# A decoder block's attention stage: probabilities turned in the order of their banks, queries requested two blocks ahead, a new written order, and the second output weights requested sooner

## The chip, the cores and the metric

The kernel runs on one core of a Trainium2 chip. The metric is the device time of one execution in microseconds (us); lower is better. Times of a kernel are medians over several runs. One execution of the kernel before was recorded by the hardware profiler, and all times of single instructions come from it.

## The reference: what is computed

One layer of a decoder block for a sequence of 2048 positions with 1024 channels, in float32. A projection feeds three groups of heads (a matrix memory, eight heads of forgetting attention, a spatial gate); their outputs are joined and multiplied by an output matrix, added to the input, and a convolutional feed-forward network follows. The change lies in the forgetting attention and in the output matrix that follows it:

```python
def forgetting_attention(q, k, v, f_pre):
    F = jnp.cumsum(jax.nn.log_sigmoid(f_pre.astype(jnp.float32)), axis=-1)
    for blk in range(s_len // Q_BLOCK):          # Q_BLOCK = 128
        lo, hi = blk * Q_BLOCK, (blk + 1) * Q_BLOCK
        logits = (jnp.einsum('bhtd,bhsd->bhts', qb, kb) * scale
                  + F[:, :, lo:hi, None] - F[:, :, None, :hi])
        logits = jnp.where(mask, logits, -jnp.inf)   # causal
        p = jax.nn.softmax(logits, axis=-1)
        outs.append(jnp.einsum('bhts,bhsd->bhtd', p, vb))
...
    y = jnp.concatenate([y_attn, y_mlstm, y_sgu], axis=-1)
    return y @ w_out
...
        x = x + gt1 * y
```

## The kernel before

The program has four stages: projections (to about 690 us of the span), attention (to 1084.6 us), the output matrix (to about 1260 us) and the feed-forward network (to the end). The change touches the second and the third.

**Attention.** Eight heads `h` of 64 channels; each has four blocks `tb` of 512 queries, worked on in the order 0 to 3 (head 0: 3, 2, with 1 and 0 done earlier; head 7: 2, 3, 0, 1). A block has four tiles `i` of 128 queries. Each step of the work is a letter of the string `order`, and the engines get their instructions in that order (a manual schedule):

- `S` (`score`): TensorE multiplies one query tile with up to 1024 keys into a pair of PSUM banks (`pair()`, three such pairs in turn, `pb` twice and `pc` once); VectorE adds the forget bias and keeps the row minimum (line 223), which writes `L`.
- `X` (`weigh`): ScalarE takes the exponential of `L` (line 231), GpSimd divides by the row sum (lines 232 and 233).
- `T`, `U`, `W` (`turn_pair`): TensorE transposes two key tiles of probabilities into a PSUM pair, 64 queries at a time, the lower half of the queries in one bank and the upper half in the other (line 246); the pair is copied to `pT` in SBUF. The letter says who copies: `T` ScalarE one half and VectorE the other, `U` ScalarE alone (line 260), `W` VectorE alone (line 262). The copy puts the two halves of each query tile side by side, in runs of 64. A pair on the diagonal (`p >= tb * 2`) is copied in two instructions, one per key tile.
- `V` (`value_pair`): two matmuls of `pT` with the values into the halves of a PSUM bank `op` (line 270).
- `Y`, `Z` (`leave`): VectorE or ScalarE copies `op` to `yo`, and SyncE writes it to two tensors in DRAM (line 286).
- `a`: one split of an output weight or of one of the joined outputs `y` into a rounded high and a low part (`split_parts`, lines 135 and 136), for the next stage.

All transfers are issued by one queue, SyncE's (SP in the profile), in the order of the program: where one has to wait for its data or its buffer, those behind it wait too. The queries of a block (`load_q`, line 189: four transfers of 128 KB) are requested at the first `S` of the block before, into four buffers `qB`, which hold two blocks. At a head's first block the keys of the next head follow them (`load_k`: four transfers of 256 KB and 1 MB of forget bias), and for each second head 1 MB of values (`load_v`).

**Output matrix.** For each block of 512 positions (`TBS`, so 2, 3, 0, 1), eight steps `j` of 24 matmuls: four row tiles with the weights' first 512 columns (`wo0`), then the same four with the second 512 (`wo1`), in the first block in that order (`by_nb`). The weights `wo0` and seven of the eight parts `y` of the first block are split during attention, by the letters `a`. Part 3 of `y`, and the weights `wo1` with their gain (`load_w(1, gt1...)`), are requested in the stage itself. All these loads go through three buffers `ld`. Four PSUM banks take the sums, so a step's sums must have been moved when the step four later begins.

Of the kernel before, what the change touches and what calls it, by code (L numbers as in the profile page):

```python
# [17 lines left out]
P = 128  # L18
# [15 lines left out]
def trunk(  # L34
# [202 lines left out]
    def turn_pair(h, tb, p, how):  # L237
        tp = pair()
        i0 = max(0, 2 * p - tb * 4)
        for j in (2 * p, 2 * p + 1):  # L240
            for i in range(max(0, j - tb * 4), 4):
                n_p = min(8, tb * 4 + i + 1 - j // 8 * 8)
                o = j // 8 * 1024 + (place(j % 8) - 4 + (n_p + 1) // 2) * P
                at = j % 2 * 256 + i * 64
                for f, r in enumerate((lower, upper)):
                    T.transpose(tp[:, f, at : at + 64], L_[h, tb, i][0][r, o : o + P], ident[r, r])
        pT = pT_[h, tb, p] = pool.tile([P, 1024], F32, name="pT", tag="pT")
        if p < tb * 2:
            src = [tp.rearrange("p f (n c) -> p f n c", c=64)]
            dst = [pT.rearrange("p (n f c) -> p f n c", f=2, c=64)]  # L250
            if how == "T":
                src, dst = [src[0][:, f] for f in range(2)], [dst[0][:, f] for f in range(2)]
        else:
            src, dst = [], []
            for j, i in ((0, i0), (1, i0 + 1)):
                src.append(tp[:, :, j * 256 + i * 64 : j * 256 + 256].rearrange("p f (i c) -> p f i c", c=64))
                dst.append(pT[:, j * 512 + i * P : j * 512 + 512].rearrange("p (i f c) -> p f i c", f=2, c=64))
        for n, (d, t) in enumerate(zip(dst, src)):
            if how == "U" or how == "T" and n == 0:
                A.copy(d, t)  # L260
            else:
                V.tensor_copy(d, t)

    def value_pair(h, tb, p):
# [3 lines left out]
        for j in (2 * p, 2 * p + 1):  # L268
            c0 = max(0, j - tb * 4) * P
            T.matmul(  # L270
                op_[h, tb][(lower, upper)[j % 2], c0:], vv_[h // 2][:, j, h % 2 * 64 : h % 2 * 64 + 64],
                pT[:, j % 2 * 512 + c0 : j % 2 * 512 + 512], start=p == 0, stop=p == 2 * tb + 1,
            )

    def leave(h, tb, how):
        op = op_.pop((h, tb))
        yo = pool.tile([P, 512], F32, name="yo", tag="yo")
        copy = V.tensor_copy if how == "Y" else A.copy
        if tb:
            copy(yo, op)  # L280
        else:
            copy(yo[lower], op[lower])
            copy(yo[upper, P:], op[upper, P:])
# [1052 lines left out]
    def y_split(n=9):  # L1336
# [6 lines left out]
        "USUSTSSUXVSSSXSVVXTXSSSVVTSSVSZUTSTYXXSVVVTUTWVXSSXSSSSXXXSVVXWTTSXUTVVTTSSSVSXSXSXSVXVSXTSXSSVXVZVT"  # L1343
        "TTSYXSUVVVTTTXZSSSTVVXVVVSSSXTSSXUVTZTSXXSSSVXXVXVSTWUSXVSTTSXUSVVWXXSSSVVXTSXSSSVXVVTUTSSSWZZXVVVVX"
        "TSSTSUSXSSZSXTVVXVTTXXSUSXVVVXVXYVSTTUSSVTTUXSSVYVXVTTSSSXVVVXVZTTTTXSSSXSVVVTTSXSSUVVXSZSSSSXSVXVTT"
        "UXSWVVVXTTTUSXSTVVXSZTXSSSVXXVSTSYSXTVVXVUTSSXSXVVVTTTSZSSXSVXVVVTUSWZUVVXSSXSXWTWXVVVVXYUSUXSSSSXXS"
        "VVXVXSTTSUVTSXSUTVTTSXSSSYVVVTXSSSSXVVVVXTTTYSSSVXXVVTTTTUVYTSSXXSXSSSXVXVVTTTSXSSXVZXVSWSVVSXXTTUSW"
        "VVTSXSSXSVVTTXSXSSSVYVUSXTTVYVVTTSXSSVVYXVSTTUSUVVYWXSXSSXaWVVWTSaVVVZSaUWWVVTTXSSSVVXSSSXVTSXSaUVXV"
        "SSaSWWaUVVaXVWSXSZTaVXaVXVTTTVVUSSSWXZXXaVXVVWaUaUVVVVTTYaUWaUVVYaVVVVZ"
# [776 lines left out]
```

## Time and profile before

| what | value |
|---|---|
| median of 3 runs | 2553.86 us (2552.37 to 2555.32) |
| the profiled execution | 2552.41 us, span 2550.4 us |
| mean granted TensorE clock | 0.992 |
| DVE (VectorE) busy | 1898.0 us (74%) |
| ACT (ScalarE) busy | 1193.5 us (47%) |
| POOL (GpSimd) busy | 382.2 us (15%) |
| packets of the data queue q1 | 45.7% of 16 engines' time |

How to read it: PE is TensorE, PEld its weight loads, SPq the queue that issues the transfers. The span is the time from the first to the last instruction. A wait is named after what ended it. An engine's idle time costs something only where others wait for it; TensorE is busy nearly all the time, so its own idle time and its slowed clock are what to look at first.

### The profile page before, as it was taken

The numbers are of one execution on the slowest core, as the hardware profiler recorded it, in microseconds if no ns is written. First come the engines' busy times: TensorE is split into PE (matmuls) and PEld (weight loads), VectorE is DVE, ScalarE is ACT, GpSimd is POOL, SyncE is SP. The second block draws the span as 40 slices with busy tenths as digits, with TensorE's granted clock in tenths as the row PEclk, the third lists the DMA queues.
The fourth block names the chain that finished last, engine by engine and source line by source line (L and its number), as shares of the span: only waits on it lengthen the run. The fifth ranks groups of instructions, "written<-read, shape, count | busy, mean of one in ns | idle before, by whom it ended". The sixth has DMA issues, their size and how long they took to land.

```text
span 2550.4 us, 39158 instructions
## 1 busy us (share of the span) xinstructions
PE 2478.5 (97%) x14361; PEld 1992.3 (78%) x14361; DVE 1898.0 (74%) x3249; ACT 1193.5 (47%) x2119; POOL 382.2 (15%) x421
## 2 busy tenths in 40 slices
PE   6999999999998989999999999999999999999999
PEld 6888888888755555578878888888888888888887
DVE  7657656576275667855599888888888888988897
ACT  5443343433376656635465444444444444444443
POOL 2023310233265455500000000000000000000000
PEclk9999999999999999999999999999999999999999
DMA  7335753455555343466723222264222219577523
GB/s 264 112 117 161 221 146 94 126 153 149 144 150 146 92 112 96 121 215 235 263 91 108 83 83 83 83 252 145 83 83 83 83 66 314 169 245 255 169 75 120
DMA packets 288792, 369.27 MB, mean 145 GB/s; under 512 B 31086, under 2 KB 181580, under 8 KB 287576
## 3 DMA queue, kind: packets, MB, share of 16 engines
q1 hardware_dynamic: 288600, 366.77, 45.7%
q8 instruction: 113, 1.85, 0.3%
q14 instruction: 79, 0.65, 0.1%
HBM read 270.15 MB, written 96.54 MB: 144 GB/s over the span
## 4 chain that ended last, share of the span: by engine, by line
PE 48%; DVE 2%; DMA 1%; ACT 1%; issue 0%; SPq 0%; POOL 0%; ACTq 0%; DVEq 0%
PE ub L54 11%; PE ub L56 11%; PE ub L55 11%; PE db L55 5%; PE db L56 5%; PE db L54 5%; DMA hc_d<-hl 1%; DMA x_d<-x 0%; DVE T L1530 0%; DVE B L1530 0%; DVE hz L1521 0%; DVE wspl L1586 0%; ACT hz L1500 0%; ACT T L1526 0%; SPq L351 0%
## 5 line engine op out<-in xcount | busy, mean ns | idle before, releaser
L54 PE MATMUL acc<-wh,hh 128*128 128x512 f32 (+2 forms) x752 | 279.6, 373 | 0.0
L54 PE MATMUL ub<-T,wsph 128*128 128x512 f32 x704 | 273.8, 389 | 1.2 <-ACT wsph L1582 1.2
L55 PE MATMUL ub<-T,wsph 128*128 128x512 f32 x704 | 274.3, 390 | 0.2 <-DVE T L1530 0.2
L56 PE MATMUL ub<-T,wspl 128*128 128x512 f32 x704 | 273.9, 389 | 0.0
L56 PE MATMUL acc<-wh,hl 128*128 128x512 f32 (+2 forms) x752 | 269.8, 360 | 0.2 <-DVE hl L596 0.2
L55 PE MATMUL acc<-wl,hh 128*128 128x512 f32 (+2 forms) x752 | 268.8, 359 | 0.6 <-DVE wl L638 0.6
L54 PE MATMUL db<-wsph 128*128 128x512 f32 x616 | 239.5, 389 | 0.0
L55 PE MATMUL db<-wspl,wsph 128*128 128x512 f32 x616 | 239.5, 389 | 0.0
L56 PE MATMUL db<-wsph,wspl 128*128 128x512 f32 x616 | 239.5, 389 | 0.0
L1582 ACT CAST wsph<-S 128x512 fp32r<-128x512 f32 x176 | 109.3, 623 | 218.8 <-PE ub L55 153.8
L55 PE MATMUL ub<-B,wsph 128*128 128x512 f32 x528 | 205.6, 389 | 1.0 <-DVE B L1530 0.9
L54 PE MATMUL ub<-B,wsph 128*128 128x512 f32 x528 | 205.7, 390 | 0.0
L56 PE MATMUL ub<-B,wspl 128*128 128x512 f32 x528 | 205.5, 389 | 0.0
L1725 ACT CAST wsph<-act 128x512 fp32r<-128x512 f32 x154 | 96.1, 624 | 229.9 <-PE db L55 219.9
L223 DVE CUSTOM_DVE_ANT_0 L<-pr,nf 128x1024 f32<-128x1024 f32 (+7 forms) x128 | 124.3, 987 | 77.7 <-PE pr L217 42.8
L217 PE MATMUL pr<-kk,q 64*128 64x512 f32 (+3 forms) x1104 | 148.0, 371 | 27.2 <-DMA q<-q_d 19.5
L231 ACT ACTIVATE L<-L,nm 128x1792 f32<-128x1792 f32 (+15 forms) x128 | 153.5, 1203 | 22.7 <-DVE nm L223 21.9
L56 PEld LDWEIGHTS acc<-wh,hl 128*128 128x128 f32 x752 | 142.4, 190 | 21.8 <-DVE hl L596 0.4
L55 PEld LDWEIGHTS acc<-wl,hh 128*128 128x128 f32 x752 | 142.9, 190 | 19.9 <-DVE wl L638 1.5
L54 PEld LDWEIGHTS acc<-wh,hh 128*128 128x128 f32 x752 | 142.8, 190 | 19.1 <-issue 0.5
L54 PEld LDWEIGHTS ub<-T,wsph 128*128 128x128 f32 x704 | 132.1, 188 | 28.8 <-ACT wsph L1582 1.6
L55 PEld LDWEIGHTS ub<-T,wsph 128*128 128x128 f32 x704 | 132.1, 188 | 28.8 <-DVE T L1530 1.6
(338 smaller groups left out, 5580.1 us busy)
## 6 DMA issues: line engine op xcount, KB each, us to landing
w<-in_w_up_dram SPq DMA_DIRECT2D x88, 512.0 KB
wd<-in_w_down_dram SPq DMA_DIRECT2D x154, 256.0 KB
wa<-in_w_ada_dram SPq DMA_DIRECT2D x96, 256.0 KB
act_d<-yc SPq DMA_DIRECT2D x44, 512.0 KB
act<-act_d SPq DMA_DIRECT2D x44, 512.0 KB
wr<-in_w_in_dram SPq DMA_DIRECT2D x64, 256.0 KB
q<-q_d SPq DMA_DIRECT2D x128, 128.0 KB
hc_d<-hl SPq DMA_DIRECT2D x28, 512.0 KB
```

Source lines behind the costliest of these rows:

```text
L54: T.matmul(ps, lh, rh, start=start, stop=False, skip_group_check=resume)
L55: T.matmul(ps, lh, rl, start=False, stop=False, skip_group_check=resume)
L56: T.matmul(ps, ll, rh, start=False, stop=stop, skip_group_check=resume)
L217: T.matmul(dst, q2[a][r, qs], kk[b][r, ks], start=n == 0, stop=n == 2 and not (last and f == own))
L223: V.tensor_tensor_reduce(out=L[:, c * 1024 : c * 1024 + w], in0=sp[:, o : o + w], in1=nf[:, c * 1024 + o : c * 1024 + o + w], scale=-1.0, ...
L231: A.activation(L, L, AF.Exp, bias=nm[:, n : n + 1], scale=-1.0, accum_out=rs)
L1582: A.copy(self.wa[p][0], self.source(p))
L1725: A.copy(hi, v)
```

## The change

Four things are changed.

- **Turning.** The transposes of a diagonal pair are packed without holes, and `pT` keeps the order of the PSUM banks: first all lower halves (512 columns), then all upper halves. Each copy is then one instruction for all letters and pairs, with long runs. The value matmuls read two runs of 256 columns (fewer on the diagonal) where they read 512 in one, and write `op` in the same order; where a diagonal pair leaves columns out, their destination is two runs. `leave` puts the halves side by side again when it copies `op` to `yo`.
- **Queries.** At a block's first `S` the queries of the next two blocks are requested, if they have not been. `qB` has six buffers and `pT` five.
- **Order.** A new string; it has 58 `T`, 69 `U` and 33 `W` where there were 100, 38 and 22, the same numbers of `S`, `X` and `V`, and one `a` more, for part 3 of `y`. All low parts of `wo0` are made by VectorE; before, GpSimd made every second.
- **Second output weights.** `load_w(1, ...)` stands behind the first step of the first block, where it stood ahead of the fifth; in the first block the parts of `y` for the second are requested from the fourth step on, two a step, where they were requested from the first on.

```diff
-            ("pT", 4096, 6), ("qB", 2048, 4), ("yo", 2048, 2),
+            ("pT", 4096, 5), ("qB", 2048, 6), ("yo", 2048, 2),
...
-        for j in (2 * p, 2 * p + 1):
-            for i in range(max(0, j - tb * 4), 4):
...
+        at, cut = {}, i0 + 1 if p >= tb * 2 else 0
+        for j in range(2):
+            for i in range(i0 + j if cut else 0, 4):
...
+                to = (j * (4 - cut) + i) * 64
...
-        pT = pT_[h, tb, p] = pool.tile([P, 1024], F32, name="pT", tag="pT")
-        if p < tb * 2:
-            src = [tp.rearrange("p f (n c) -> p f n c", c=64)]
-            dst = [pT.rearrange("p (n f c) -> p f n c", f=2, c=64)]
-            if how == "T":
-                src, dst = [src[0][:, f] for f in range(2)], [dst[0][:, f] for f in range(2)]
+        pT = pT_[h, tb, p] = pool.tile([P, 2, 512], F32, name="pT", tag="pT")
+        cs = slice(i0 * 64, (8 - cut) * 64)
+        if how == "T":
+            A.copy(pT[:, 0, cs], tp[:, 0, cs])
+            V.tensor_copy(pT[:, 1, cs], tp[:, 1, cs])
         else:
...
+            (A.copy if how == "U" else V.tensor_copy)(pT[:, :, cs], tp[:, :, cs])
...
-                op_[h, tb][(lower, upper)[j % 2], c0:], vv_[h // 2][:, j, h % 2 * 64 : h % 2 * 64 + 64],
-                pT[:, j % 2 * 512 + c0 : j % 2 * 512 + 512], start=p == 0, stop=p == 2 * tb + 1,
+                op_[h, tb][r].rearrange("p (f n) -> p f n", f=2)[:, :, c0:], vv_[h // 2][:, 2 * p + j, h % 2 * 64 : h % 2 * 64 + 64],
+                pT[:, :, to + c0 : to + 256], start=p == 0, stop=p == 2 * tb + 1,
...
+        src, dst = op.rearrange("p (f i c) -> p f i c", f=2, c=64), yo.rearrange("p (i f c) -> p f i c", f=2, c=64)
         if tb:
-            copy(yo, op)
+            copy(dst, src)
...
-        "USUSTSSUXVSSSXSVVXTXSSSVVTSSVSZUTSTYXXSVVVTUTWVXSSXSSSSXXXSVVXWTTSXUTVVTTSSSVSXSXSXSVXVSXTSXSSVXVZVT"
+        "TSUSUSXSUXVSSSUVSXUXSVSSSXSVVVXSTZTSXSVVSZTUWVSXXSUXSTXVVSSSVVXXWXTTSXUWVVTTZXSSVSXSVSXSUVXSSUVVSUUY"
...
-    w_list = [("w", k) for k in range(KT)] + [("y", k) for k in (0, 1, 2, 4, 5, 6, 7)]
+    w_list = [("w", k) for k in range(KT)] + [("y", k) for k in (0, 1, 2, 4, 5, 6, 7, 3)]
...
-                if n + 1 < len(heads):
-                    load_q(*heads[n + 1], "qB")
+                for q in heads[n + 1 : n + 3]:
+                    if q not in qs_:
+                        load_q(*q, "qB")
...
-                wo.append(split_parts(*got, "wo0", (G, V)[k % 2]))
+                wo.append(split_parts(*got, "wo0", V))
...
-    y_load(0, 3)
-    y_split()
...
-            if (n, j) == (0, 4):
+            blk.mm(i, nb)
+            if (n, j) == (0, 0):
                 load_w(1, gt1[:, 512:1024])
-            blk.mm(i, nb)
...
-                for k in {5: (5, 6), 6: (7,), 7: ()}.get(j, (j,)):
+                for k in ({3: (0, 1), 4: (2, 3), 5: (4, 5), 6: (6, 7)}.get(j, ()) if n == 0 else {5: (5, 6), 6: (7,), 7: ()}.get(j, (j,))):
```

SyncE's queue at the start of head 5, before. The first two rows are the queries of its block 1 (`q_10684` and `q_10687`), then come keys and bias for head 6, the values, a written-out block, and the queries of block 2 (`q_10866` and `q_10869`):

```order
L189 DMA q_10684<-q_d_60 64x512 x2
L189 DMA q_10687<-q_d_60 64x512 x2
L174 DMA kk_10690<-k_d_61 64x1024 x2
L174 DMA kk_10691<-k_d_61 64x1024 x2
L175 DMA nf_10692<-nf_d_63 128x2048
L182 DMA vv_10698<-v_d_62 128x512 x4
L286 DMA yt_d_68<-yo_10817 64x512
L286 DMA y2_d_69<-yo_10817 64x512
L189 DMA q_10866<-q_d_60 64x512 x2
L189 DMA q_10869<-q_d_60 64x512 x2
```

The same place of the changed kernel. Here `q_10680` and `q_10683` are the queries of block 2, and `q_10796` and `q_10799` those of block 3:

```order
L189 DMA q_10680<-q_d_60 64x512 x2
L189 DMA q_10683<-q_d_60 64x512 x2
L174 DMA kk_10686<-k_d_61 64x1024 x2
L174 DMA kk_10687<-k_d_61 64x1024 x2
L175 DMA nf_10688<-nf_d_63 128x2048
L182 DMA vv_10694<-v_d_62 128x512 x4
L282 DMA yt_d_68<-yo_10774 64x512
L282 DMA y2_d_69<-yo_10774 64x512
L189 DMA q_10796<-q_d_60 64x512 x2
L189 DMA q_10799<-q_d_60 64x512 x2
```

The queries of block 2 have moved ahead of keys, bias and values; those of block 3 stand where block 2's stood.

SyncE's queue at the start of the output matrix, before: `yt_d` and `y_d` are the two tensors of joined outputs, `x` rows of the input, and the last row is the eight requests for the second output weights.

```order
L298 DMA ld<-y_d 128x512
L1462 DMA x_13426<-in_x_dram 128x1024
L294 DMA ld<-yt_d 128x512
L1462 DMA x_13466<-in_x_dram 128x1024
L298 DMA ld<-y_d 128x512
L294 DMA ld<-yt_d 128x512
L1462 DMA x_13714<-in_x_dram 128x1024
L1462 DMA x_13819<-in_x_dram 128x1024
L298 DMA ld<-y_d 128x512
L294 DMA ld<-in_w_out_dram 128x512 x8
```

The same place of the changed kernel, from the last blocks written out by attention (`yo`) on, with `gt` the gains:

```order
L290 DMA ld<-in_w_out_dram 128x512 x2
L282 DMA yt_d<-yo 64x512
L282 DMA y_d<-yo 64x512
L290 DMA ld<-in_w_out_dram 128x512
L282 DMA yt_d<-yo 64x512
L282 DMA y_d<-yo 64x512
L1419 DMA gt_13286<-gt_d 128x1024
L1459 DMA x_13288<-in_x_dram 128x1024
L1459 DMA x_13372<-in_x_dram 128x1024
L1459 DMA x_13404<-in_x_dram 128x1024
L290 DMA ld<-in_w_out_dram 128x512 x2
```

The first three of the eight weight requests now stand ahead of attention's last writes, and no `y` of the second block stands between them.

More of the change, by code (lines that the diff above doesn't have):

```diff
@@ L239, in turn_pair @@
         i0 = max(0, 2 * p - tb * 4)
[L240 to L262 removed]
+        at, cut = {}, i0 + 1 if p >= tb * 2 else 0
+        for j in range(2):
+            for i in range(i0 + j if cut else 0, 4):
+                n_p = min(8, tb * 4 + i + 1 - p // 4 * 8)
+                o = p // 4 * 1024 + (place((2 * p + j) % 8) - 4 + (n_p + 1) // 2) * P
+                to = (j * (4 - cut) + i) * 64
+                for f, r in enumerate((lower, upper)):
+                    T.transpose(tp[:, f, to : to + 64], L_[h, tb, i][0][r, o : o + P], ident[r, r])
+        pT = pT_[h, tb, p] = pool.tile([P, 2, 512], F32, name="pT", tag="pT")
[3 more added lines that the diff above has]
+            V.tensor_copy(pT[:, 1, cs], tp[:, 1, cs])
+        else:
+            (A.copy if how == "U" else V.tensor_copy)(pT[:, :, cs], tp[:, :, cs])
     def value_pair(h, tb, p):
@@ L1354, in trunk @@
     v_list, x_list, y_list, parts = list(t_list), [], [], []
-    w_list = [("w", k) for k in range(KT)] + [("y", k) for k in (0, 1, 2, 4, 5, 6, 7)]
+    w_list = [("w", k) for k in range(KT)] + [("y", k) for k in (0, 1, 2, 4, 5, 6, 7, 3)]
     def request():
-        while w_list and sum(2 if q == ("y", 0) or q == ("y", 1) or q == ("y", 2) else 1 for q, _ in parts + [(w_list[0], 0)]) <= 3:
+        while w_list and sum(1 + (q[0] == "y" and q[1] < 4) for q in [q for q, _ in parts] + w_list[:1]) <= 3:
             q = w_list.pop(0)
```

23 lines of the change are left out of this document (13 added, 10 removed).

## The prediction, made before the changed kernel was run

> **What bounds the kernel now.** I read the share of each engine first, then the windows by stage, then who TensorE waits for in the stages that change, and last the queue that brings what it waits for.
>
> ```profile
> PE 2478.5 (97%) x14361; PEld 1992.3 (78%) x14361; DVE 1898.0 (74%) x3249; ACT 1193.5 (47%) x2119; POOL 382.2 (15%) x421
> core 0: us, PE busy (x) PEld busy (x) DVE busy (x) ACT busy (x) POOL busy (x), PEclk, DMA share, GB/s
> 690.00:1084.60 394.60, 359.06 (x4127) 227.31 (x4126) 268.08 (x542) 250.49 (x428) 213.43 (x244) 0.97 0.43 120
> 1084.60:1130.00 45.40, 41.09 (x166) 32.71 (x165) 25.84 (x42) 14.64 (x30) 0.00 (x0) 0.92 0.67 222
> 1130.00:1230.00 100.00, 99.80 (x471) 82.72 (x470) 62.96 (x113) 43.94 (x87) 7.73 (x11) 1.00 0.71 244
> ```
>
> TensorE is busy 97% of the span. Of its 2550.4 − 2478.5 = 71.9 us of idle time, 394.60 − 359.06 = 35.5 lie in attention and 4.3 in the first 45 us of the output matrix; behind that it does not pause (99.80 of 100 us). The other engines have room in attention: VectorE 268 of 395 us, ScalarE 250, GpSimd 213. So a change here pays by TensorE's pauses, and by its clock, which is below 1 in just these two rows. What ends the pauses:
>
> ```profile
> PE pr L217 <- DMA q<-q_d: 19.5, 6, 7.3
> PE pr L217 <- DVE pT L262: 7.0, 18, 0.5
> PE wps L54 <- ACT wo1h L135: 3.1, 1, 3.1
> PE pr L246 <- DVE pT L262: 4.9, 12, 1.3
> PE wps L54 <- ACT yhl L135: 1.2, 1, 1.2
> ```
>
> (Total us, times, longest.) Six waits for queries are 19.5 of the 35.5 us. They are long; the others in attention are many and short.
>
> **Queries.** The longest of the six, first on SyncE's queue, then on TensorE:
>
> ```profile
> 913.53 2.47 SPq L189 DMA_DIRECT2D q<-q_d  x4
> 916.05 3.05 SPq L174 DMA_DIRECT2D kk<-k_d  x4
> 919.14 0.58 SPq L175 DMA_DIRECT2D nf<-nf_d  x1
> 919.77 2.75 SPq L182 DMA_DIRECT2D vv<-v_d  x4
> 923.13 0.59 SPq L286 DMA_DIRECT2D y_d<-yo  x1
> 924.09 26.75 SPq L189 DMA_DIRECT2D q<-q_d  x12
> 931.45 2.18 PE L217 MATMUL pr<-kk,q 64*128 64x512 f32 x6 [7.30 <-DMA q<-q_d]
> ```
>
> The first four transfers are the queries of block 1 of head 5. Behind them stand 3 MB of keys, bias and values, and only then, at 924.09, the queries of block 2. TensorE had run out at 931.45 − 7.30 = 924.15: block 1 is four scores, so nothing lies between its start and the need for block 2. The six waits stand once in each of the heads 1 to 6, always at block 2.
>
> After, the queries of block 2 are requested at the start of block 0, ahead of the 3 MB; those of block 3 take the place behind it. In the new order at least 15 scores, turns and value pairs lie between the start of block 0 and block 2 (head 2), and at least 29 between block 1 and block 3 (head 5). The stage has 504 such steps in 359 busy us, 0.71 us each: 10.7 and 20.7 us. The request for block 3 needs what block 2's needs now, 931.45 − 924.09 = 7.4 us. Both are covered, if not by much for the first. **All six waits go: −19.5 us.** That the new requests wait for a buffer is excluded: six hold three blocks, and the third was read to its end when the request is made.
>
> **The clock.** The windows that begin where TensorE resumes, and one behind the shortest of these waits over a microsecond (1.88 us, at 735.39):
>
> ```profile
> 735.00:740.00 5.00, 4.61 (x35) 2.85 (x35) 2.62 (x5) 3.25 (x7) 4.47 (x6) 1.00 0.26 78
> 776.40:783.20 6.80, 6.75 (x22) 3.37 (x22) 1.23 (x2) 0.00 (x0) 2.16 (x3) 0.52 0.21 64
> 827.10:830.90 3.80, 3.71 (x12) 1.81 (x14) 1.68 (x3) 0.00 (x0) 2.62 (x4) 0.55 0.51 142
> 931.40:936.80 5.40, 5.36 (x17) 2.91 (x18) 1.23 (x2) 0.00 (x0) 0.00 (x0) 0.52 0.30 87
> 974.30:981.10 6.80, 6.76 (x26) 3.34 (x28) 1.80 (x4) 0.00 (x0) 4.68 (x9) 0.51 0.99 273
> 1111.20:1117.70 6.50, 6.43 (x16) 5.04 (x17) 6.12 (x10) 2.60 (x6) 0.00 (x0) 0.52 0.49 157
> 735.39 1.98 PE L217 MATMUL pr<-kk,q 64*128 64x512 f32 x10 [1.88 <-DMA q<-q_d]
> 974.34 2.11 PE L217 MATMUL pr<-kk,q 64*128 64x384 f32 x6 [2.44 <-DMA q<-q_d]
> ```
>
> Behind the wait of 1.88 us the granted clock stays 1.00; behind those of 2.44 us and more it is about half, while TensorE is busy throughout. What is lost is length times missing clock: 6.8 × 0.48 + 3.8 × 0.45 + 5.4 × 0.48 + 6.8 × 0.49 = 10.9 us in attention, and 6.5 × 0.48 = 3.1 us in the output matrix. **−10.9 us here.**
>
> The Trainium skill ("TensorE: Matmul & The Clock Gate", part 1) says that the clock halves after an idle window of some 3.4 us and is whole again after one busy window of that length. By that figure each of five drops would cost 1.7 us, 8.5 in all in place of 14.0, and the sum below would end at 2520 (an estimate from that page). The rows show 3.8 to 6.8 us at half speed, and a drop behind a wait of 2.44 us, so the rows are used.
>
> **Second output weights.** At 1107.78 the first four steps end, and the fifth waits for `wo1h`:
>
> ```profile
> 1107.78 0.39 PE L56 MATMUL wps<-wo0h,yhl 128*128 128x512 f32 x1
> 1104.74 15.01 SPq L294 DMA_DIRECT2D ld<-in_w_out_dram  x8
> 1110.60 0.62 ACT L135 CAST wo1h<-ld 128x512 fp32r<-128x512 f32 x1
> 1111.27 1.22 PE L54 MATMUL wps<-wo1h,yhl 128*128 128x512 f32 x2 [3.11 <-ACT wo1h L135]
> ```
>
> The requests stood behind parts of `y` that went through the same three buffers, and were issued 20 us into the stage. In the new order three are issued ahead of attention's last writes. At the pace seen here (eight in 15.0 us, and the first one's cast done 1110.60 + 0.62 − 1104.74 = 6.5 us after its request) the last is ready some 21.5 us into the stage. The fifth step comes 1108.2 − 1084.6 − 1.2 = 22.4 us into it, and reads the last weight most of a step later. **−3.1 us and −3.1 us of clock.** The parts of `y` for the second block, 12 transfers through the same buffers, now come in the last four steps. At 1.9 us each (15.0 / 8) they take 23 us; four steps are 22.4 us, and the last part is read most of another step later. I put this at 0; were it late, it could give back the 6.2 us just gained. That the splits of `wo0` all go to VectorE costs nothing on TensorE: VectorE has 126 idle us in attention.
>
> The wait of 1.2 us for `yhl` was part 3 of `y`, which is now made during attention, ahead of the last four value pairs: **−1.2 us.**
>
> **Turning.** The copies:
>
> ```profile
> L260 ACT COPY pT<-pr 128x512 f32<-128x512 f32 x85 | 48.0, 588 | 74.7 <-PE pr L246 73.6
> L260 ACT COPY pT<-pr 128x1024 f32<-128x1024 f32 x25 | 25.4, 1017 | 11.7 <-PE pr L246 11.4
> L262 DVE COPY pT<-pr 128x512 f32<-128x512 f32 x67 | 44.4, 688 | 26.6 <-ACT pT L260 26.5
>   DVE pT L262: 57.0, 64
> L280 DVE COPY yo<-op x11: 681/685/690, 753.3 to 1079.4; 128x512 f32<-128x512 f32 x11
> L231 ACT ACTIVATE L<-L,nm 128x2048 f32<-128x2048 f32 x8 | 16.0, 2003 | 1.6 <-DVE nm L223 1.5
> ```
>
> Long runs save nothing on a copy: VectorE takes 688 ns for 512 columns that it lays down in pieces of 64 (`pT`), and 685 for 512 in one run (`yo`, as it is before). What could matter is the fourth row, from the view of line 260: 64 times VectorE's half of a `T` waited for ScalarE's, 57.0 us in all. So a `T` frees its PSUM pair after 588 and then 688 ns, one behind the other, and a `U` after 1017. This wait stands in the changed program too, but `T` falls from 100 to 58. That may shorten TensorE's short waits (7.0 + 4.9 us for `pT`); on the other side 69 copies, not 38, are ScalarE's alone, and may stand behind exponentials of up to 2.0 us (the last row). I take 0. Bounds: the best stretch without a wait for queries, 1000 to 1050,
>
> ```profile
> 1000.00:1050.00 50.00, 48.82 (x561) 29.75 (x558) 41.60 (x78) 34.62 (x50) 31.07 (x29) 1.00 0.34 91
> ```
>
> has 1.18 idle us in 50, or 8.6 in 365; the short waits are 35.5 − 19.5 = 16.0 now, so −7.4. On the other side they could double: +16.0.
>
> **The matmuls** of `V` now read two runs 512 columns apart, and on the diagonal write two runs. A matmul that reads four runs of 64 columns exists (line 778), and the contiguous kind beside it:
>
> ```profile
> 213.44 1.02 PE L778 MATMUL trp<-sv,wT 128*128 128x256 f32 x4
> 1072.29 2.79 PE L270 MATMUL op<-pT,vv 128*64 128x512 f32 x12
> L270 PE MATMUL op<-pT,vv 128*64 128x512 f32 (+3 forms) x640 | 143.9, 560 | 1.4 <-ACT pT L260 1.4
> ```
>
> Four records of 256 columns in 1.02 us are 1.00 ns a column; the value matmuls run two at a time, and 12 records of 512 in 2.79 us are 0.91 ns a column of a pair. Nearly the same, and the first includes the tail of a short run: reading in pieces is free. Writing in two runs is not shown. I take 0; the price of a doubled matmul is the 143.9 us.
>
> **Sum.** 19.5 + 10.9 + 3.1 + 3.1 + 1.2 = 37.8 us. The profiled execution took 2552.4 us, its span and 2.0 around it; the median shown is 1.4 above. 2552.4 − 37.8 = 2514.6, and I say 2515.
>
> **The rivals.**
> (1) *The next engine is late.* With the long pauses gone, ScalarE and VectorE have no time to catch up, and the pair banks come free late. For it: the 11.9 us of waits for `pT` that are there already, more `U` behind exponentials of up to 2.0 us. Against it: the stretch from 1000 on, where TensorE is 98% busy with VectorE at 41.60 of 50. Price: up to the 16.0 above, so 2531. Chance 0.15.
> (2) *The request doesn't come sooner.* SyncE works in order, and its waits for blocks to be written out are long:
>
> ```profile
> SPq L286 <- DVE yo L280: 48.6, 9, 12.4
> ```
>
> If such a wait (12.4 us at the longest) stood ahead of most of the new requests, the 10.7 us of cover would be gone, and only the output matrix would gain: 2552.4 − 7.4 = 2545. Against it: at 913.53 the request followed at once on the write ahead of it. Chance 0.05.
> (3) *Slower: the value matmuls pay for their pieces.* If reading or writing in two runs costs TensorE time, it falls on 640 records and 143.9 us, with nothing beside it. It decides from 37.8 / 143.9 = 26% on; a doubling gives 2552.4 − 37.8 + 143.9 = 2658. Line 778 speaks against it for reads; for writes nothing does. Chance 0.04. The Trainium skill ("Advanced Engine Details and Errata", PSUM Cachelines) says that any non-contiguous pattern slows matmuls significantly, and asks that each two elements lie together, which runs of 64 and more do; the write is what no row here can check.
>
> **How the numbers follow.** The forecast holds from 2505 (2514.6 − 7.4, and 2 of spread) to 2525 (the short waits up by half, or the second block's `y` late): 0.72. With (1) at 0.15, to 2537. (2) 0.05, (3) 0.04, and 0.04 that gains and losses cancel. A measurement of this kernel can tell 0.2%, 5 us, from no change; (1) and (2) are on the faster side, so faster 0.92, the same 0.04, slower 0.04. The range, 2505 to 2537, leaves out (2), (3) and the cancelling.
>
> **What would show it.** No wait of line 217 for `q` over a microsecond; granted clock 1.00 over attention and the start of the output matrix; the wait for `wo1h` gone; about 16 us of short waits in attention; the records of the value matmuls at 560 ns in the mean, and the stage some 30 us shorter. Wrong would be: waits for `q` that remain at block 2, value matmuls with longer records, or waits for `pT` near 30 us.

## The result, and the profile after

| | before | after |
|---|---|---|
| median, us | 2553.55 (2552.37 to 2555.32) | **2511.55** (2509.33 to 2512.56) |
| ratio | | 0.9834, 95% interval 0.9817 to 0.9851 |
| profiled execution, us | 2552.41 | 2511.05 |
| its span, us | 2550.4 | 2509.3 |
| attention ends at (first `wps` matmul) | 1084.30 | 1049.39 |
| output matrix, from there to the first `ub` matmul | 194.0 | 189.2 |
| from there to the end of the span | 1272.0 | 1270.7 |

The changed kernel is 1.7% faster. Of the 41.0 us that the span lost, 34.9 lie in attention, 4.8 in the output matrix and 1.3 behind it, where nothing was changed. The share of each engine, the first line of the page after:

```profile
PE 2464.3 (98%) x14361; PEld 1985.6 (79%) x14361; DVE 1888.1 (75%) x3206; ACT 1200.8 (48%) x2100; POOL 377.6 (15%) x417
```

TensorE has the same 14361 instructions and 2509.3 − 2464.3 = 45.0 us of idle time, where it had 71.9. The windows by stage after, with the columns shown before (length; busy time of PE, PEld, DVE, ACT, POOL; granted clock, DMA share, GB/s). The first is attention, the second and third are the 45.4 and the 100 us behind its end:

```profile
690.00:1049.40 359.40, 347.79 (x4126) 221.16 (x4124) 259.90 (x501) 257.93 (x409) 209.43 (x240) 1.00 0.46 132
1049.40:1094.80 45.40, 45.40 (x201) 37.61 (x201) 26.33 (x44) 13.97 (x29) 1.10 (x2) 1.00 0.71 230
1094.80:1194.80 100.00, 96.80 (x456) 79.99 (x456) 65.48 (x116) 46.74 (x93) 5.90 (x9) 1.00 0.74 256
```

In attention the idle time is 359.40 − 347.79 = 11.6 us, where it was 35.5, and the busy time is 11 us shorter for the same number of matmuls: most of that is the clock, now 1.00 where it was 0.97. The output matrix begins without a pause (45.40 of 45.40). But the next 100 us, which had 0.2 us of pauses, now have 3.2. Who TensorE waits for from 690 to 1400, after (total us, times, longest):

```profile
PE pr L247 <- ACT pT L254: 4.1, 2, 2.8
PE op L265 <- ACT pT L254: 3.2, 2, 2.8
PE tps L1496 <- ACT hz L1497: 2.5, 3, 1.8
PE pr L217 <- DVE pT L252: 2.4, 10, 0.5
PE tps L1496 <- DVE x L1488: 1.4, 1, 1.4
PE pr L247 <- ACT vt L798: 0.8, 1, 0.8
PE op L265 <- DVE pT L252: 0.5, 1, 0.5
```

Waits for `q`, for `wo1h` and for `yhl` are gone. The short waits for VectorE's `pT` (11.9 us before) are 3.1. Two kinds have grown: a few longer waits for ScalarE's `pT` (7.3 us; 1.4 before), and waits of the output matrix's transposes `tps` (3.9 us). Of these, before had 2.0:

```profile
PE tps L1499 <- DVE x L1491: 1.1, 1, 1.1
PE tps L1499 <- ACT hz L1500: 0.9, 3, 0.5
```

The transposes of the last block stand behind the first `ub` matmul, in the next stage. Within the output matrix itself the waits for `tps` are 3.2 us, where they were 0.2.

SyncE's queue at the start of head 5, after:

```profile
889.14 2.38 SPq L189 DMA_DIRECT2D q<-q_d  x4
891.58 3.52 SPq L174 DMA_DIRECT2D kk<-k_d  x4
895.20 0.53 SPq L175 DMA_DIRECT2D nf<-nf_d  x1
895.77 1.91 SPq L182 DMA_DIRECT2D vv<-v_d  x4
899.54 8.82 SPq L189 DMA_DIRECT2D q<-q_d  x8
```

The transfers ahead of the 3 MB are now block 2's; those behind it are for block 3 and later, and TensorE waited for none.

The two longest of the new waits, on TensorE, and what ScalarE did just ahead of each:

```profile
994.16 2.38 PE L247 MATMUL pr<-ident,L 64*128 64x64 f32 x48 [2.80 <-ACT pT L254]
1047.34 1.07 PE L265 MATMUL op<-pT,vv 128*64 128x512 f32 x4 [2.80 <-ACT pT L254]
```

```profile
992.57 0.62 ACT L135 CAST wo0h<-ld 128x512 fp32r<-128x512 f32 x1 [4.13 <-DMA ld<-in_w_out_dram]
993.10 1.01 ACT L254 COPY pT<-pr 128x1024 f32<-128x1024 f32 x1
1045.86 0.62 ACT L135 CAST yhl<-ld 128x512 fp32r<-128x512 f32 x1 [3.32 <-DMA ld<-yt_d]
1046.39 0.90 ACT L254 COPY pT<-pr 128x896 f32<-128x896 f32 x1
```

ScalarE works in order. It stood 4.13 and 3.32 us at a cast (letter `a`) whose load had not landed, and the copy that TensorE needed stood behind it. Both are splits for the next stage, which have time; the letter's place makes them urgent.

### The profile page after: what moved, and what is told of

Read it like the earlier page. It is cut to its first block, busy times and chain, and to the rows that moved or that the text cites. A ratio compares the mean times of both kernels' runs of the same rounds, so it can differ in the third digit from the quotient of the medians.

```text
span 2509.3 us, 39058 instructions
## 1 busy us (share of the span) xinstructions
PE 2464.3 (98%) x14361; PEld 1985.6 (79%) x14361; DVE 1888.1 (75%) x3206; ACT 1200.8 (48%) x2100; POOL 377.6 (15%) x417
## 4 chain that ended last, share of the span: by engine, by line
PE 49%; DVE 2%; DMA 1%; ACT 1%; issue 0%; SPq 0%; POOL 0%; ACTq 0%; DVEq 0%
PE ub L54 11%; PE ub L55 11%; PE ub L56 11%; PE db L55 6%; PE db L54 6%; PE db L56 6%; DMA hc_d<-hl 1%; DMA x_d<-x 0%; DVE T L1527 0%; DVE B L1527 0%; DVE hz L1518 0%; DVE wspl L1583 0%; ACT hz L1497 0%; ACT T L1523 0%; ACT yg L1476 0%
## 5 line engine op out<-in xcount | busy, mean ns | idle before, releaser
L56 PEld LDWEIGHTS ub<-T,wspl 128*128 128x128 f32 x704 | 132.2, 188 | 27.7 <-DVE wspl L1583 0.3
```

The costliest lines, as they stand in the source:

```text
L56: T.matmul(ps, ll, rh, start=False, stop=stop, skip_group_check=resume)
```

## The experiments

Twelve runs were made in four sessions, each beside the kernel before on the same chip. From the profile of each (one execution), by the marks of the table above:

| run | time, us | ratio (95%) | attention ends | output matrix |
|---|---|---|---|---|
| two_ahead | 2516.52 | 0.9849 (0.9835 to 0.9864) | 1054.44 | 191.3 |
| one_ahead | 2520.12 | 0.9862 (0.9847 to 0.9877) | 1057.97 | 191.1 |
| late_w1 | 2510.47 | 0.9821 (0.9806 to 0.9836) | 1046.76 | 190.2 |
| layout_alone | 2553.29 | 0.9992 (0.9982 to 1.0003) | 1088.72 | 192.0 |
| after_again | 2507.62 | 0.9825 (0.9809 to 0.9841) | 1045.83 | 189.3 |
| better_splits | 2512.13 | 0.9841 (0.9824 to 0.9858) | 1049.73 | 190.2 |
| old_layout | 2509.87 | 0.9833 (0.9816 to 0.9850) | 1046.32 | 191.4 |
| soon_w1 | 2550.81 | 0.9995 (0.9984 to 1.0006) | 1088.14 | 191.0 |
| splits_moved | 2506.33 | 0.9816 (0.9803 to 0.9829) | 1043.78 | 191.9 |
| scale_first | 2510.55 | 0.9828 (0.9814 to 0.9841) | 1047.32 | 190.7 |
| both | 2508.75 | 0.9826 (0.9813 to 0.9840) | 1045.32 | 190.6 |
| old_mix | 2512.97 | 0.9838 (0.9825 to 0.9852) | 1050.97 | 189.5 |

How far such numbers can be trusted is in the table. `after_again` is the changed kernel itself and came out 3.9 us below its first time; before, `layout_alone` and `soon_w1` are nearly the same in attention and end it at 1084.30, 1088.72 and 1088.14. The output matrix of `before`, `layout_alone` and `two_ahead` is the same program, and took 194.0, 192.0 and 191.3 us. So some 4 us between two single profiles, or between two sessions, say nothing, and 2 to 3 us of the output matrix say nothing either.

**two_ahead: the queries alone.** The kernel before with the requests two blocks ahead; a second tag takes every other block, so that `pT` keeps its six buffers.

```diff
-                if n + 1 < len(heads):
-                    load_q(*heads[n + 1], "qB")
+                for m in (n + 1, n + 2):
+                    if m < len(heads) and heads[m] not in qs_ and (m == n + 1 or heads[m][0] < NH - 1):
+                        load_q(*heads[m], "qA" if m % 2 and heads[m][0] < NH - 1 else "qB")
```

> The kernel before with one thing changed: the queries of a block are requested two blocks ahead (blocks of heads 0 to 6 take the buffers qA and qB in turn, so that no buffer is taken from pT). Theory (the waits for queries and the clock they cost): no wait of line 217 for q above 1 us, granted clock 1.00 in attention, 19.5 + 10.9 = 30 us less, so 2523 (2518 to 2530). Rival (the new written order brings the gain, early requests alone only move the waits to the PSUM pairs): 2540 to 2554, with waits for pT above 25 us.

Measured: 2516.52 us, a little below the expected range; before had 2553.81 in the same session, so this alone is worth 37.3 us. Its attention, and TensorE's waits there:

```profile
690.00:1054.44 364.44, 347.38 (x4130) 223.44 (x4128) 267.71 (x542) 250.01 (x427) 213.35 (x244) 1.00 0.47 128
PE pr L217 <- DVE pT L262: 7.5, 21, 0.5
PE pr L246 <- DVE pT L262: 4.9, 11, 1.6
PE op L270 <- ACT pT L260: 2.3, 1, 2.3
```

Attention ends 1084.30 − 1054.44 = 29.9 us sooner; the prediction's two terms make 19.5 + 10.9 = 30.4. The other 7 us are not explained: 2.7 of them lie in the output matrix, where this kernel changes nothing, and the profiled execution, at 2519.70, was the slowest of its four. The busy time is at once what it is in the changed kernel (347.38 against 347.79): the clock comes back with the queries, but for one drop in each of the two. The waits for VectorE's `pT` are what they were (7.0 and 4.9 before), so the next engine did not become late.

**one_ahead: the changed kernel without the second block.**

```diff
-                for q in heads[n + 1 : n + 3]:
+                for q in heads[n + 1 : n + 2]:
```

> The changed kernel with the queries requested one block ahead, as before. Theory: waits for queries come back at block 2 of the heads; in the new order more work stands between blocks 1 and 2 (13 steps in head 5 instead of 4), so some 10 us of waits and some 5 us of clock: 2527 (2520 to 2536). Rival (the order brings the gain): within 3 us of the changed kernel, 2509 to 2515.

Measured: 2520.12 us. TensorE's first line of waits, from 690 to 1060:

```profile
PE pr L217 <- DMA q<-q_d: 5.7, 4, 3.7
```

The waits are back, but four and not six, and 5.7 us and not the 10 that were expected: the new order alone already puts more work between block 1 and block 2 (in head 5, 9 scores, turns and value pairs instead of 4). So the two parts overlap. Beside the changed order, the second block is worth only 2520.1 − 2511.6 or − 2507.6, 8.5 to 12.5 us, which is neither the 16 of the theory nor the nothing of its rival.

**layout_alone and old_layout: the turning.** The first is the kernel before with the new `turn_pair`, `value_pair` and `leave`; the second is the changed kernel with the three old ones. For `value_pair`, the core of `layout_alone`:

```diff
-                op_[h, tb][(lower, upper)[j % 2], c0:], vv_[h // 2][:, j, h % 2 * 64 : h % 2 * 64 + 64],
-                pT[:, j % 2 * 512 + c0 : j % 2 * 512 + 512], start=p == 0, stop=p == 2 * tb + 1,
+                op_[h, tb][r].rearrange("p (f n) -> p f n", f=2)[:, :, c0:], vv_[h // 2][:, 2 * p + j, h % 2 * 64 : h % 2 * 64 + 64],
+                pT[:, :, to + c0 : to + 256], start=p == 0, stop=p == 2 * tb + 1,
```

> The kernel before with turned probabilities in the order of their banks, and nothing else. Theory (long runs are no faster to copy, and pieces cost the matmuls nothing): 2553.5 within 4 us, the records of the value matmuls at 560 ns in the mean. Rivals: writing or reading in two runs costs TensorE time, over 2558 with longer records; or one copy instead of two on the diagonal frees ScalarE and VectorE, 2540 to 2548.

> The changed kernel with the turned probabilities in the old layout, everything else kept. Theory (the layout is worth nothing by itself): 2511.5 within 3 us. Rival (with 47 of the diagonal pairs copied by one engine, two copies instead of one cost some 0.2 us each on ScalarE or VectorE, and TensorE waits for them): 2515 to 2521, with more waits of TensorE for pT.

Measured: 2553.29 us, ratio 0.9992, and 2509.87 us, between the two times of the changed kernel. The value matmuls of `layout_alone`:

```profile
L265 PE MATMUL op<-pT,vv 128*64 128x512 f32 (+3 forms) x640 | 144.9, 563 | 1.5 <-ACT pT L254 1.5
```

144.9 us and 563 ns a record, where it was 143.9 and 560 in whole runs. That mean mixes shapes. All records read two runs, but only the 192 shorter ones, on the diagonal, write two. One of their three shapes, in the changed kernel and in `old_layout`, which has the same order:

```profile
L265 PE MATMUL op<-pT,vv 128*64 128x384 f32 x64 | 27.0, 504 | 0.0
L270 PE MATMUL op<-pT,vv 128*64 128x384 f32 x64 | 27.0, 504 | 0.0
```

The other two, of 256 and 128 columns, take 393 and 287 ns in both kernels. Reading and writing in two such runs is free, and so the new layout neither costs nor gives anything that can be measured, with either order.

**late_w1 and soon_w1: the second output weights.** `late_w1` is the changed kernel with the old places of these requests (part 3 of `y` stays in attention); `soon_w1` is the kernel before with the new places alone. The diff of `soon_w1`; that of `late_w1` is the reverse:

```diff
-            if (n, j) == (0, 4):
+            blk.mm(i, nb)
+            if (n, j) == (0, 0):
                 load_w(1, gt1[:, 512:1024])
-            blk.mm(i, nb)
...
-                for k in {5: (5, 6), 6: (7,), 7: ()}.get(j, (j,)):
+                for k in ({3: (0, 1), 4: (2, 3), 5: (4, 5), 6: (6, 7)}.get(j, ()) if n == 0 else {5: (5, 6), 6: (7,), 7: ()}.get(j, (j,))):
```

> The changed kernel with the second output weights and the parts of y of the second block requested where they were before. Theory: the wait for wo1h (3.1 us) and the halved clock behind it (3.1 us) come back: 2518 (2515 to 2520). Rival (attention ends earlier and leaves room, so the wait does not come back): 2511.5.

> The kernel before with the second output weights requested sooner and the parts of y of the second block later, and nothing else (part 3 of y stays where it was). Prediction's step: the wait for wo1h and its clock go, 6.2 us less than before, 2547.5. Theory after late_w1 (what is gained there is given back at the transposes of the first blocks, whose scaling stands behind splits that wait for their loads): 0 to 3 us less, 2550.5 to 2553.8, with the transposes' waits at 3 us and more instead of 2.0.

Measured: 2510.47 us, not slower than the changed kernel, where the theory asked for 2515 at the least, and 2550.81 us, ratio 0.9995. TensorE's waits in the output matrix, first of `late_w1`, then of `soon_w1`:

```profile
PE wps L54 <- ACT wo1h L135: 2.8, 2, 2.6
PE tps L1496 <- ACT hz L1497: 0.8, 2, 0.5
PE tps L1496 <- DVE x L1488: 0.7, 1, 0.7
```

```profile
PE tps L1499 <- DVE x L1491: 2.4, 1, 2.4
PE tps L1499 <- ACT hz L1500: 1.8, 3, 1.0
```

The wait for `wo1h` comes back in `late_w1` and goes in `soon_w1`: it follows the place of the request, as it was meant to. But in `soon_w1` the transposes `tps` then wait 4.2 us in all, where it was 2.0 (1.5 in `late_w1`). A part of the gain is taken back further on in the same stage.

**after_again, better_splits and splits_moved: where the splits stand.** `after_again` is the changed kernel once more. The other two move letters `a` from places where their load had not landed to others, and give the first request a letter of its own, `r`, so that it no longer stands right ahead of a split. Order of `splits_moved` (its last two rows; `better_splits` has the same new letter and other places):

```diff
-        "ZSSTXVVWTSSXVVWXUSSXVSSUVXYVVSUXSVWSUTVSSSXUYVSSXTXVVSYWTXXaVUVVSTaaVVUWaTaVVUaUVUSVZSSSXXSaVaVVUSSX"
-        "UXVSVSSSWWXXVSUZaVVVXUSXSUWVSXXWXUaVVUTVSWXUXaVYaVUWaVaVVUZWaVVUZUaVVVVZ"
+        "ZSSTXVVWTSSXVVWXUSSXVSSUVXYVVSUXSVWSUTVSSSXUYVSSXTXVVSYWTXXrVUVVSTaaVVUWaTaVVUaUVUSVaZSSSXXSaVaVVUSS"
+        "XUXVSVSSSWWXXVSUZaVVVXUSXSUWVSXaXWXUVVUTaVSWXUXaVYaVUWaVaVVUZWVVUZUaVVVVZ"
```

> The changed kernel itself, for a second profile and beside the next three on one chip: 2511.5 within 3 us. The waits behind the splits (on ScalarE's copies, 7.3 us in the first profile) show whether they are fixed by the order (then they stand at the same places again) or by chance of the transfers.

> The changed kernel with the splits moved: the first loads are requested at the first letter a, and split some 5 us later; splits of the tail stand earlier, so that fewer casts stand ahead of ScalarE's copies while their load is on its way. Theory (the remaining long waits, 2.8 + 1.3 + 2.8 us, come from casts that wait for a load ahead of the copies TensorE needs): 5 to 8 us less than the changed kernel with its clock, 2503 to 2507. Rival (the loads' wait is only moved to the first matmuls of the output matrix): within 2 us of it.

> As better_splits, but no split stands ahead of a score whose load cannot have come: the split that made the wait of 4.2 us there goes back to its old place, two of the tail go forward. Theory (TensorE's long waits that remain in attention are casts and splits that wait for a load ahead of work TensorE needs): attention ends 3 to 5 us earlier than in the second profile of the changed kernel (1045.8), no wait over 1.5 us in it; 2503 to 2506. Rival (each split that is moved makes a wait elsewhere): 2507 to 2512.

Measured: 2507.62, 2512.13 and 2506.33 us. In `after_again` TensorE waits behind the casts at the same first two places, 994.46 and 1041.41, but for 1.42 and 1.64 us where the first profile had 2.80 and 1.31; the third wait is gone. So the order fixes the places, and the landing of the loads, which varies, fixes the lengths. All waits for ScalarE's `pT` together are 3.5 us instead of 7.3, which is about what this profile gains in attention.

`better_splits` took the old waits away and made a new one:

```profile
1016.10 1.01 PE L217 MATMUL pr<-kk,q 64*128 64x256 f32 x6 [4.16 <-DVE nm L223]
1016.00:1023.00 7.00, 6.90 (x68) 4.98 (x70) 4.35 (x13) 2.65 (x5) 3.42 (x4) 0.54 0.01 4
```

This is 4.16 us of pause, and 7 us at a clock of 0.54 behind it (the second row, a window). A split of `y` now stood ahead of a score's bias on VectorE. It did not wait for its load there, as the expectation of `splits_moved` has it; its two instructions were slow, while GpSimd was dividing:

```profile
1009.91 2.02 DVE L299 TENSOR_TENSOR ld<-ld 128x512 f32<-128x512 f32 x1
1012.61 2.23 DVE L136 TENSOR_TENSOR yhl<-ld,yhl 128x512 fp32r<-128x512 f32 x1 [0.68 <-ACT yhl L135]
1012.43 1.87 POOL L233 TENSOR_SCALAR L<-L,rs 128x1920 f32<-128x1920 f32 x1
```

Of the twenty such instructions from 690 to 1060 us in this profile, the 13 beside which GpSimd did not divide took 0.69 us at most; of the other 7, five took 1.0 to 2.2 us. `splits_moved` is free of that wait: no wait in attention is over 1 us, and attention ends at 1043.78, the soonest of all. What it won is lost again in its output matrix (191.9 us, against 189.2 and 189.3), where `tps` waits:

```profile
PE tps L1496 <- ACT hz L1497: 3.0, 4, 1.3
PE tps L1496 <- DVE x L1488: 2.2, 1, 2.2
```

Its median lies just above the range of its theory (2503 to 2506). It is the lowest of all runs, but 1.3 us below `after_again` from another session: that it beats the changed kernel isn't shown.

**scale_first and both: the waits of the transposes.** `x` is scaled in place by VectorE (line 1488) before it is transposed. The two longest waits for `tps` in the profile after, at 1152.87 and 1161.77, are those of the second block. The last scaling ahead of them, and what comes before it on VectorE and on SyncE's queue:

```profile
1145.02 0.69 DVE L299 TENSOR_TENSOR ld<-ld 128x512 f32<-128x512 f32 x1 [1.80 <-DMA ld<-y_d]
1147.06 0.69 DVE L1475 TENSOR_TENSOR x<-wps,x 128x512 f32<-128x512 f32 x1
1152.07 0.75 DVE L1488 TENSOR_SCALAR x<-x,st 128x1024 f32<-128x1024 f32 x1 [0.65 <-DMA x_d<-x]
```

```profile
1147.78 0.32 SPq L1478 DMA_DIRECT2D x_d<-x  x1
```

The scaling waits for `x` to be written out. SyncE's queue does not hold this write up: it is issued at 1147.78, as soon as the last sum has been added to `x` (line 1475, done at 1147.75). What is late is this addition. Its sum was ready some 7 us before, but ahead of it on VectorE stand splits of `y` for the fourth block, which wait for their loads (the first row). In both kernels the scaling is put ahead of the splits of `y` in the first step of each block but the first; only in the step behind the first block is the written order made binding (a manual schedule). `both` has the order of `splits_moved` as well.

```diff
+            if (n, j) == (1, 0):
+                short = ExitStack()
+                short.enter_context(tc.manual_schedule())
+            if (n, j) == (1, 1):
+                short.close()
...
-            y_split()
+            early = n > 0 and j == 0
+            if not early:
+                y_split()
...
+            if early:
+                y_split()
+                some({1: 2, 2: 5, 3: 3}.get(n, 0))
```

> The changed kernel with the last row tile of the first block scaled ahead of the splits of y for the third block (a short stretch in written order, which also moves some of the instructions behind it). Theory (the transposes' waits of 3.8 and 3.9 us, where the gain of the sooner second weights went, come from the scaling that stands behind a split waiting for its load): these waits fall to 1 us or less, the output matrix takes 186.5 to 188 us in place of 189.2, and the time 2505 to 2509. Rival (they come from the transfers of x or from the stage's load as a whole): waits and time as they are.

> splits_moved and scale_first together. Theory: the sum of the two, 2500 to 2505. Rival: no faster than the changed kernel.

Measured: 2510.55 and 2508.75 us, with 4.5 and 4.1 us of waits for `tps`. They did not go, but the edit did not reach them: the waits belong to the second block, and there VectorE's order is as it was. In `scale_first`:

```profile
1149.76 0.69 DVE L299 TENSOR_TENSOR ld<-ld 128x512 f32<-128x512 f32 x1 [1.41 <-DMA ld<-y_d]
1151.19 0.69 DVE L136 TENSOR_TENSOR yhl<-ld,yhl 128x512 fp32r<-128x512 f32 x1 [0.74 <-ACT yhl L135]
1151.80 0.75 DVE L1488 TENSOR_SCALAR x<-x,st 128x1024 f32<-128x1024 f32 x1
```

The scaling still stands right behind a split, and the addition ahead of it still comes 6.6 us after its sum. So these two runs say nothing for the splits as the cause of the waits, and nothing against it.

**old_mix: the letters or their sequence.** The changed kernel with 42 of its `U` and `W` turned to `T` again, evenly spread, so that the counts are those of before. The first row of the order:

```diff
-        "TSUSUSXSUXVSSSUVSXUXSVSSSXSVVVXSTZTSXSVVSZTUWVSXXSUXSTXVVSSSVVXXWXTTSXUWVVTTZXSSVSXSVSXSUVXSSUVVSUUY"
+        "TSUSTSXSUXVSSSTVSXUXSVSSSXSVVVXSTZTSXSVVSZTTWVSXXSUXSTXVVSSSVVXXTXTTSXTWVVTTZXSSVSXSVSXSUVXSSUVVSTUY"
```

> The changed kernel with its new order, in which 31 of the 69 U and 11 of the 33 W, evenly spread, are T again: 100 T, 38 U and 22 W, as before the change. Nothing else differs. Theory (a T frees its PSUM pair in two copies one behind the other, and fewer T are what shortened TensorE's short waits): the waits for VectorE's pT, 3.1 us in attention after the change and 12 before, are back at 9 to 14 us, attention ends 5 to 10 us later than at 1045.8 to 1049.4, and the kernel takes 2514 to 2520 us. Rival (the sequence of the steps, with shorter bursts of turns, is what did it, and the letters do not matter): the waits for pT stay at 3 to 5 us, attention ends between 1045 and 1050, and the time is 2507 to 2512 us. If it is slower than 2520 us, the T stand where ScalarE or VectorE was full, and the test says nothing of the old order.

Measured: 2512.97 us; attention ends at 1050.97. TensorE's waits from 690 to 1090:

```profile
PE pr L247 <- DVE pT L252: 3.9, 5, 2.2
PE pr L217 <- DVE pT L252: 2.4, 11, 0.5
PE op L265 <- DVE pT L252: 1.5, 2, 1.1
```

The waits for VectorE's `pT` are 7.8 us, between the 3.1 of the changed kernel and the 11.9 of before. But half of them are the waits behind casts under another name. The longest, and what stood ahead of it on ScalarE and VectorE:

```profile
997.73 2.31 PE L247 MATMUL pr<-ident,L 64*128 64x64 f32 x48 [2.21 <-DVE pT L252]
995.73 0.62 ACT L135 CAST wo0h<-ld 128x512 fp32r<-128x512 f32 x1 [3.13 <-DMA ld<-in_w_out_dram]
996.38 0.69 DVE L136 TENSOR_TENSOR wo0l<-ld,wo0h 128x512 fp32r<-128x512 f32 x1 [4.37 <-ACT wo0h L135]
```

It is the place that is 994.16 in the profile after. The turn there is now a `T`, so VectorE's half is the one that comes last. The other two places have waits of 0.68 and 1.06 us. Without these three, 3.9 us are left, which is what the rival asked for, and the waits of line 217 are 2.4 us as in the changed kernel, where before had 7.0. Attention ends 1.6 us later than the latest of the five profiles of the changed order (1045.8 to 1049.4). So it is the sequence of the steps that shortened the short waits, and hardly the letters; neither the end of attention nor the time can tell the letters from nothing.

## Why the prediction was right, by its own steps

The forecast was 2515 and the change gave 2511.55: 42.0 us where 38.5 were expected. The main mechanism was right in place and size; two smaller terms were off, in opposite directions, and that they partly cancel is luck.

| step | forecast, us | measured, us | from |
|---|---|---|---|
| queries | −19.5 | −19.5 | six waits, none left |
| clock in attention | −10.9 | −11.0; −9.2 by the granted clock | busy time 358.8 to 347.8; one drop left |
| turning and order | 0 (−7.4 to +16.0) | −4.4, and −8.3 in `after_again` | the rest of the idle time |
| second weights, their clock, part 3 of `y` | −7.4 | −4.8 (one pair of profiles) | output matrix 194.0 to 189.2 |
| matmuls in two runs | 0 | 0 | `layout_alone` |

**Queries.** Right, and shown: `two_ahead` alone took the waits away, shortened attention by 29.9 us and the kernel by 37.3, and in `one_ahead` waits of the same kind came back. That the requests might come no sooner (rival 2) is answered by the rows from 889.14 on.

**The clock.** Right, and shown by the same run. The busy time fell by 11.0 us after, by 11.4 in `two_ahead` and by 10.7 in `after_again`; the windows of before summed to 10.9. Of the three only `after_again` has no drop left in attention. The other two have one each, behind the waits at 994.16 and 1045.98: 3.4 us at half speed, so 1.7 lost, and the granted clock accounts for 9.2 us there. The agreement to 0.1 us is chance; to 2 us it is shown. Here a page and the rows differed. By an estimate from the figure of the Trainium skill ("TensorE: Matmul & The Clock Gate", part 1) each drop costs 1.7 us, 6.8 for the four in attention.

**Turning, and the order.** This is the term that was too small. The idle time of attention fell by 35.5 − 11.6 = 23.9 us (27.8 in `after_again`), of which the queries are 19.5. The rest, 4.4 to 8.3 us, is a balance: of the 11.9 us for VectorE's `pT`, 3.1 are left, while the waits for ScalarE's rose from 1.4 to 7.3 us (3.5 in `after_again`). The value taken was 0, and in `after_again` the gain reaches the bound of 7.4 drawn from the best stretch of before. The layout has no part in it (`old_layout` ends attention at 1046.32), and the queries have none (`two_ahead` still waits 12.4 us for VectorE's `pT`). What is left is the order string with its splits. Fewer `T` are not what does it: in `old_mix`, with 100 `T` again, all but 0.8 us of the short waits stayed away. Which trait of the sequence does it, shorter bursts of turns or another, was not tested. What the all-VectorE splits of `wo0` do, and five buffers `pT` instead of six, was not tried alone either.

Rival 1, that the next engine is late, did not come as it was put, with 16.0 us more. Its mechanism did show, in a small way: the waits for ScalarE's `pT` rose from 1.4 to 7.3 us. They came behind casts that waited for a load, not behind exponentials as that rival had it.

**Second output weights.** This term was too large. The wait for `wo1h` went, with its clock, as worked out, though the last weight was cast 24.1 us into the stage and not 21.5. The step that failed is another: it took both for a gain of the whole stage, and asked only whether the parts of `y` for the second block would be late. They are not; no matmul of `wps` waits in the profile after. What TensorE meets instead, a block further on, are its own transposes. Within the output matrix the waits for `tps` are 0 to 0.2 us in the profiles with the old places (before, `layout_alone`, `two_ahead`, `late_w1`), and 2.0 to 4.5 us in all ten with the new. With the old places TensorE reaches the transposes of the second block 107 to 110 us into the stage, and the last scaling that they need is done at 106 to 109. With the new places it is there at 102 to 104, but that scaling is done only at 103 to 107. Much of the time won at `wo1h` is spent there: VectorE, and ScalarE with the copies of `tps`, are held by splits for the fourth block that wait for their loads. That these splits are the cause is read from the traces, and no run tests it.

With the rest of the change in place, the new places give nothing that can be told: 2510.47 us with the old ones, 2511.55 and 2507.62 with the new. Alone, they give a ratio of 0.9995 (0.9984 to 1.0006). The 4.8 us of the table are one pair of profiles, and the unchanged stage alone differs by 2.7.

**Part 3 of `y`.** Right: the wait of 1.2 us is gone in every kernel that makes it in attention.

**Matmuls in two runs.** Right, and rival 3 is out for this shape. The Trainium skill ("Advanced Engine Details and Errata", PSUM Cachelines) warns of any non-contiguous pattern. With runs of 64 columns or more, read and written, this case shows no cost: 563 ns a record where it was 560 in the order of before, and 547 in both layouts in the new order.

## What to carry to other kernels

Where one queue issues all transfers in order, look at what stands ahead of a small urgent request: here 3 MB that could wait stood ahead of 512 KB that TensorE needed at once, and asking for it one block sooner took 30 us off attention, and alone 37 of the 42 us off the time. Count a pause together with the slowed clock behind it, which here added half as much again. And a cast for a later stage, written into the order of an engine that also serves TensorE, is harmless only once its load has landed; when one such wait is moved away, look where the next appears, since twice here it only changed its place. And when a wait in front is taken away, ask which engine TensorE then runs into: much of the gain at `wo1h` went to the transposes of the next block.

## What the runs showed of the hardware that was not expected

The same pause does not always cost clock. Behind the two waits of 2.80 us shown above, the clock was different:

```profile
994.10:997.50 3.40, 3.34 (x52) 2.61 (x54) 3.36 (x6) 3.28 (x7) 0.00 (x0) 0.60 0.38 109
1047.30:1050.70 3.40, 2.96 (x14) 1.49 (x15) 1.54 (x3) 2.52 (x5) 0.00 (x0) 1.00 0.48 146
```

Behind the first it fell to half for about 3.4 us, behind the second not at all. The traces record each change of the clock. All stretches at half speed in attention and the output matrix last 3.41, 6.83 or 10.24 us (the one of 10.24 begins within the pause of 7.30 us, so 5.1 of it lie behind). The length does not follow the pause: before, that of 2.44 us was followed by 6.8 us, and the wait for `wo1h` (2.4 to 3.1 us) by 6.8 us before and by 3.4 in `late_w1`.

The changes lie on a grid. Before, the clock falls at 776.16, 827.36, 926.35, 974.13 and 1110.66 us, and these times are 15, 29, 14 and 40 steps of 3.413 us apart; within each of the fourteen profiles all changes of the clock fit such a grid to 5 ns. So there are windows of 3.413 us that run on, whatever TensorE does, and it matters how a pause falls across them. The pause that ended at 994.16 lies in one window, from 991.40 to 994.81, with 2.76 us idle. The one that ended at 1047.34 is split between two, with 1.48 and 1.73 us idle. Counted over all fourteen profiles from 690 to 1300 us, outside the stretches at half speed: the clock fell behind each of the 26 windows with 2.02 us idle or more, behind 5 of the 29 with 1.26 to 2.00, and behind none with less.

The VectorE instructions of a split, which read two operands from SBUF, can take three times as long while GpSimd divides: 2.02 and 2.23 us in place of 0.69 in `better_splits`, as shown above.

The copies of the two halves of a `T` still follow one another, though each reads a PSUM bank of its own and writes a half of `pT` of its own: in the profile after, the groups of line 252 show that VectorE waits for ScalarE.

```profile
L252 DVE COPY pT<-pr 128x512 f32<-128x512 f32 x41 | 27.6, 688 | 34.9 <-ACT pT L251 34.8
```

41 of these copies waited 34.8 us for ScalarE's half. Whether the program or the chip asks for that was not looked into.
